# Weight pieces that move in natural-orientation products start 64 bytes later in their buffers

## The chip, the cores and the metric

The kernel runs on one core of a Trainium2 chip. The metric is the device time of one execution in microseconds (us), as the median of several runs. A profile of one execution shows what each engine did: TensorE (PE for matmuls, PEld for the loading of a stationary operand), VectorE (DVE), ScalarE (ACT), GpSimd (POOL), SyncE (SP), and the DMA queues.

## The reference

The reference is a two-layer encoder trunk in float32 on 256 tokens of width 2048. Cut to what matters here:

```python
for layer in range(2):
    h = rmsnorm(x, attn_norm[layer])
    if layer == 0:      # two head groups: chunked attention, differential attention
        qa, ka, va, qb, kb, vb = split(h @ even_w_in)          # 2048 x 6144
        x = x + concat(attn_a(qa, ka, va), attn_b(qb, kb, vb)) @ even_w_out
    else:               # sparse attention on a shared latent c (256 wide), 16 heads
        q, cl, ... = split(h @ odd_w_in); c = rmsnorm(cl)
        # keys of a head are c @ w_uk, its values c @ w_uv
        x = x + attn_c(q, c, w_uk, w_uv) @ odd_w_out
    h = rmsnorm(x, ffn_norm[layer])
    x = x + (silu(h @ w_gate) * (h @ w_up)) @ w_down           # inner width 5632
return rmsnorm(x, final_norm)
```

Nearly all the work is the product of 256 tokens with some 390 MB of float32 weights.

## The kernel before, in words

**Weights in pieces.** A weight matrix comes as pieces of 128 partitions by 1024 columns: two row blocks (j = 0 and 1) of 512 columns each. `sources` is a generator that yields the pieces in the order of their use, and `load_w` takes the next one: SyncE's queue loads it into a buffer `wl` (5 of them), ScalarE writes its rounded copy `wh` in the format float32r, VectorE the remainder `wo = wl - wh`. Of `wh` and of `wo` there are 3 buffers each. `next_w` keeps three pieces ahead. The activations stand in the same split form: `xs` (the normalized input, 16 blocks), `mix` (attention output), `y` (inner activations of the FFN), `c` (the latent), each block as a high half and a low half of 256 tokens.

**Two kinds of product.** In `gemm_t`, `products` makes transposed outputs: the weights are stationary (128 columns are loaded into the array) and the activations move through it. Per piece and output block n this is a group of four matmuls: `wh` of j = 0 and 1 against the high and low halves at once (512 columns move), then `wo` of j = 0 and 1 against the high half (256 columns move). The projections of queries and keys, both output projections, and all of the FFN are made so. In `keys_values` the keys of layer 1 (`uk`) are made in the same way from `w_uk`, with the latent `c` as the moving operand.

In `gemm_n` the outputs are in natural orientation (tokens on partitions; the tile is called `nat`): here 128 tokens of the activations are stationary and the weights move, 512 columns at a time, in three matmuls: activation high by `wh`, high by `wo`, low by `wh`. Only values are made so: the third group of `even_groups` of each of the four head quads of layer 0 (8 pieces each, with `xs`), and `w_uv` in layer 1 (4 pieces, with `c`).

**Order.** The program of PE is a fixed list, written in the order of these calls. Between the matmuls of a gemm `pump` places small steps of the attention. A matmul that 512 columns move through is preceded by a load of its stationary operand, which overlaps the matmul before it.

**Addresses.** Tiles lie at fixed offsets within each partition, in the order in which they are allocated. In the program as built, `xs` begins at byte 32,896, the three `wh` at 89,664 and every 4096 bytes after it, the three `wo` at 101,952 and every 4096 bytes after it. Tiles called `spacer` (88, 8 and 168 floats) move `y` and `mix` to chosen offsets: `y` is at 123,008, `mix` at 180,352 in layer 0 and 170,112 in layer 1; `c` is at 221,376. The slices that the matmuls take start at multiples of 512 bytes from these, except in the small projection `x` (pieces of 656 columns), where those of j = 1 start 1312 bytes in.

Of the kernel before, what the change touches and what calls it, by code (L numbers as in the profile page):

```python
# [14 lines left out]
F32R = mybir.dt.float32r  # L15
# [5 lines left out]
P = 128  # L21
S = 256
D = 2048
KT = D // P
# [15 lines left out]
def encoder_kernel(  # L40
# [25 lines left out]
    wpool = ctx.enter_context(tc.tile_pool(name="wpool", bufs=1))  # L66
# [14 lines left out]
        return psum.tile(shape, F32, name=name, tag="ps")  # L81


    OUT0 = [4, 5, 6, 7, 0, 1, 2, 3]
    QUADS = (2, 3, 0, 1)

    def even_groups(quad):
        return (quad, 2 + quad, 4 + quad) if quad < 2 else (4 + quad, 6 + quad, 8 + quad)

    def ffn_sources(layer):  # L90
        for g in range(FT // 4):
            yield from (w_gate[layer, g, k] for k in range(KT // 2))
            yield from (w_up[layer, g, k] for k in range(KT // 2))
        for g in range(4):
            yield from (w_down[layer, g, k] for k in range(FT // 2))

    def sources():
        for quad in QUADS:
            for g in even_groups(quad):
                yield from (w_ein[g, k] for k in range(KT // 2))  # L100
        for g in range(4):
            yield from (w_eout[g, k] for k in OUT0)
        yield from ffn_sources(0)
        yield from (w_ox[k] for k in range(KT // 2))
        yield from (w_oi[k] for k in range(KT // 2))
        for quad in range(4):
            yield from (w_oq[quad, k] for k in range(KT // 2) if quad)
            yield w_uk[quad]
            yield w_uv[quad]
            yield from (w_oq[quad, k] for k in range(KT // 2) if not quad)  # L110
        for g in range(4):
            yield from (w_oout[g, k] for k in range(KT // 2))
        yield from ffn_sources(1)

    stream = sources()
    ahead = deque()
    latest = {}
    before = deque()

    def load_w(cuts=1, between=None):  # L120
        src = next(stream, None)
        if src is None:
            return
        if before:
            before.popleft()()
        width = src.shape[-1]
        wl = wpool.tile([P, width], F32, name="wl", tag="wl", bufs=5)
        wh = wpool.tile([P, width], F32R, name="wh", tag="wh", bufs=3)
        wo = wpool.tile([P, width], F32R, name="wo", tag="wo", bufs=3)
        for i in range(cuts):  # L130
            if between is not None:
                between(i)
            c = slice(i * width // cuts, (i + 1) * width // cuts)
            nc.sync.dma_start(out=wl[:, c], in_=src[:, c])
            latest["act"] = nc.scalar.activation(wh[:, c], wl[:, c], AF.Copy)  # L135
            nc.vector.tensor_tensor(out=wo[:, c], in0=wl[:, c], in1=wh[:, c].bitcast(F32), op=ALU.subtract)  # L136
        ahead.append((wh, wo))

    def next_w():
        while len(ahead) < 3:  # L140
            n = len(ahead)
            load_w()
            if len(ahead) == n:
                break
        return ahead.popleft()
# [188 lines left out]
    def load_x(t, n):  # L334
        if t:
            nc.sync.dma_start(out=xt[:, t:t + n, :], in_=xT[:, t:t + n, :])
        normalize_tiles(t, n, 0)

    load_w(2, between=lambda i: load_x(i, 1))
    before.extend(partial(load_x, t, 2) for t in range(2, KT, 2))  # L340
    load_w(2)
    load_w(2)

# [3 lines left out]
    def attention_pools(stack, spacer):  # L347
        ap = stack.enter_context(tc.tile_pool(name="attn", bufs=2))
        mixp = stack.enter_context(tc.tile_pool(name="mix", bufs=1))
        mixp.tile([P, spacer], F32, name="spacer")  # L350
        return ap, mixp, mixp.tile([P, KT, 2, S], F32R, name="mix")
# [134 lines left out]
    stack = ExitStack()  # L486
    ap, mixp, mix = attention_pools(stack, 8)
# [55 lines left out]
    for quad in QUADS:  # L543
        qk, ps = {}, []
# [31 lines left out]
    def out_proj(mix, order, gi):  # L576
        st = {"acc": None}
        for g in range(4):
            banks = gemm_t(mix, KT, order)
            if g == 0:  # L580
                drain()
            add_residual(banks, 4 * g, gi, st)
        return st

    st = out_proj(mix, OUT0, 1)
    stack.close()
# [75 lines left out]


    stack = ExitStack()
    ap, mixp, mix = attention_pools(stack, 168)
    hk = mixp.tile([P, C_HEADS, S], F32, name="hk1")
    steps.append(norm_steps(st, "n2", scale))

# [127 lines left out]
    for quad in range(4):  # L796
        qk = {}
# [89 lines left out]
```

## Time and profile before

| what | us |
|---|---|
| median of 3 runs | 2138.07 (2137.47 to 2138.16) |
| the profiled execution's own time | 2138.02 |
| its span, from first to last instruction | 2136.2 |
| PE busy with matmuls | 2122.6 |
| VectorE busy | 1347.7 |
| ScalarE busy | 1067.7 |

The profiled execution's time is its span and 1.8 us around it. The granted clock of TensorE is 0.998 of full speed over the span. The duration that the profile shows for one matmul is longer than its share of the engine's time, since a matmul starts while the one before it drains; how often one starts is read from the starts in the timeline. A row of the timeline joins matmuls that follow one another on the same tiles: its first number is the start of the first of them.

### The profile page before, as it was taken

What the parts mean: (1) busy time and instruction counts of PE and PEld (TensorE: products, weight loads), DVE (VectorE), ACT (ScalarE), POOL (GpSimd) and SP (SyncE); (2) the same over time, 40 slices, a digit from 0 to 9 for tenths busy, and PEclk for the clock granted to TensorE, in tenths of its full rate; (3) what the DMA queues carried; (4) which work ended last, traced back from release to release, by engine and by line L of the source; (5) the groups of instructions that cost most, each with busy time, mean ns of one, the idle gap of its engine ahead of it and who ended that gap; (6) DMA issues with size and microseconds to landing.
All of it is one profiled execution on the core that took longest, in us unless ns stands there. A gap on an engine that the chain in (4) does not pass through costs nothing.

```text
span 2136.2 us, 31865 instructions
## 1 busy us (share of the span) xinstructions
PE 2122.6 (99%) x12280; PEld 1862.8 (87%) x12280; DVE 1347.7 (63%) x1978; ACT 1067.7 (50%) x1575; POOL 231.0 (11%) x232
## 2 busy tenths in 40 slices
PE   9999999999999999999999999999999999999998
PEld 8888888888888888888888888888888888888887
DVE  6665557766666666655547977666666666654444
ACT  6555555545454544444435566454454545444442
POOL 3111001100000000000002242110010000100000
PEclk9999999999999999999999999999999999999999
DMA  8455445555555555555556444655555555555553
GB/s 288 163 179 177 168 168 187 189 195 188 190 193 190 190 194 188 192 192 187 180 185 214 164 160 147 198 188 190 195 188 192 192 189 193 191 189 193 191 190 127
DMA packets 114407, 398.92 MB, mean 187 GB/s; under 512 B 12554, under 2 KB 16718, under 8 KB 114254
## 3 DMA queue, kind: packets, MB, share of 16 engines
q1 hardware_dynamic: 114110, 396.75, 56.0%
q8 instruction: 96, 1.57, 0.3%
q14 instruction: 57, 0.47, 0.1%
q10 hardware_dynamic: 144, 0.13, 0.0%
HBM read 394.70 MB, written 2.14 MB: 186 GB/s over the span
## 4 chain that ended last, share of the span: by engine, by line
PE 95%; DVE 2%; POOL 1%; ACT 1%; issue 1%; DMA 1%; SPq 0%; POOLq 0%; DVEq 0%; ACTq 0%
PE acc L171 86%; PE nat L171 4%; PE x L171 1%; DVE wo L136 1%; DMA xt<-in_xT 1%; POOL sqacc L299 1%; PE uk L171 0%; DVE sc L748 0%; DVE sc L758 0%; ACT wh L135 0%; POOL tm L767 0%; DVE m L757 0%; DVE xt L818 0%; PE c3o L171 0%; DVE qT L318 0%
## 5 line engine op out<-in xcount | busy, mean ns | idle before, releaser
L136 DVE TENSOR_TENSOR wo<-wl,wh 128x1024 fp32r<-128x1024 f32 (+2 forms) x747 | 943.6, 1265 | 727.4 <-ACT wh L135 718.1
L135 ACT ACTIVATE wh<-wl 128x1024 fp32r<-128x1024 f32 (+2 forms) x747 | 785.1, 1051 | 897.1 <-PE acc L171 821.6
L171 PE MATMUL acc<-xs,wh 128*128 128x512 f32 x3648 | 1139.4, 393 | 0.2 <-ACT wh L135 0.2
L171 PEld LDWEIGHTS acc<-xs,wo 128*128 128x128 f32 x3648 | 685.1, 188 | 152.5 <-DVE wo L136 2.0
L171 PE MATMUL acc<-xs,wo 128*128 128x256 f32 x3648 | 722.8, 279 | 1.0 <-DVE wo L136 1.0
L171 PEld LDWEIGHTS acc<-xs,wh 128*128 128x128 f32 x3648 | 554.4, 188 | 3.2 <-ACT wh L135 0.9
L171 PE MATMUL acc<-y,wh 128*128 128x512 f32 x1412 | 437.1, 391 | 0.0
L171 PEld LDWEIGHTS acc<-y,wo 128*128 128x128 f32 x1408 | 264.4, 188 | 58.1
L171 PE MATMUL acc<-y,wo 128*128 128x256 f32 x1408 | 278.3, 279 | 0.0
L171 PEld LDWEIGHTS acc<-y,wh 128*128 128x128 f32 x1412 | 213.8, 188 | 0.0
L171 PE MATMUL acc<-mix,wh 128*128 128x512 f32 x512 | 160.0, 394 | 0.0
L317 ACT ACTIVATE u<-acc 128x256 f32<-128x256 f32 x228 | 86.2, 378 | 60.8 <-PE acc L171 55.8
L171 PEld LDWEIGHTS acc<-mix,wo 128*128 128x128 f32 x512 | 96.1, 188 | 21.3
L171 PE MATMUL acc<-mix,wo 128*128 128x256 f32 x512 | 101.1, 279 | 0.0
L299 POOL TENSOR_TENSOR sqacc<-sqacc,sq 128x512 f32<-128x512 f32 (+1 forms) x36 | 53.4, 1483 | 410.3 <-ACT sq L294 408.2
L171 PE MATMUL nat<-wh,xs 128*128 128x512 f32 x256 | 83.6, 394 | 0.0
L606 POOL TENSOR_TENSOR ga<-ga,n1rs 128x256 f32<-128x256 f32 x44 | 36.6, 843 | 425.4 <-DVE ga L605 411.3
L606 POOL TENSOR_TENSOR ga<-ga,n3rs 128x256 f32<-128x256 f32 x44 | 36.6, 843 | 425.5 <-DVE ga L605 411.2
L171 PEld LDWEIGHTS acc<-mix,wh 128*128 128x128 f32 x512 | 77.7, 188 | 0.2
L171 PEld LDWEIGHTS nat<-wh,xs 128*128 128x128 f32 x256 | 48.0, 187 | 10.8
L305 DVE TENSOR_TENSOR xt<-acc,xt 128x256 f32<-128x256 f32 x120 | 44.6, 418 | 19.1 <-PE acc L171 19.1
L171 PE MATMUL nat<-wo,xs 128*128 128x512 f32 x128 | 50.5, 394 | 0.0
(811 smaller groups left out, 1084.7 us busy)
## 6 DMA issues: line engine op xcount, KB each, us to landing
wl<-in_w_gate SPq DMA_DIRECT2D x176, 512.0 KB, 3.3
wl<-in_w_up SPq DMA_DIRECT2D x176, 512.0 KB, 3.3
wl<-in_w_down SPq DMA_DIRECT2D x176, 512.0 KB, 3.3
wl<-in_w_ein SPq DMA_DIRECT2D x93, 512.0 KB, 3.3
wl<-in_w_eout SPq DMA_DIRECT2D x32, 512.0 KB, 3.3
wl<-in_w_oq SPq DMA_DIRECT2D x32, 512.0 KB, 3.2
wl<-in_w_oout SPq DMA_DIRECT2D x32, 512.0 KB, 3.4
wl<-in_w_oi SPq DMA_DIRECT2D x8, 512.0 KB, 4.3
```

The source lines that it names most:

```text
L135: latest["act"] = nc.scalar.activation(wh[:, c], wl[:, c], AF.Copy)
L136: nc.vector.tensor_tensor(out=wo[:, c], in0=wl[:, c], in1=wh[:, c].bitcast(F32), op=ALU.subtract)
L171: nc.tensor.matmul(out, a, b, start=start, stop=stop, skip_group_check=True)
L299: nc.gpsimd.tensor_tensor(out=st["acc"][:, :n, :], in0=st["acc"][:, :n, :], in1=sq[:, :n, :], op=ALU.add)
L305: nc.vector.tensor_tensor(out=xt[:, t0 + i, :], in0=b[:, part, :], in1=xt[:, t0 + i, :], op=ALU.add)
L317: nc.scalar.activation(u[:m], b[:m, 0, :], AF.Copy)
L606: nc.gpsimd.tensor_tensor(out=a, in0=a, in1=st["rs"], op=ALU.mult)
```

## The change

A piece that `sources` marks gets an offset of 16 floats (64 bytes) within its `wh` and `wo` buffers; each of these buffers grows by 32 floats (128 bytes) so that it has room for that. The marked pieces are the value pieces of layer 0 (the third group of each quad) and `w_uk`. `w_uv` is not marked. The spacer ahead of `mix` in layer 1 falls from 168 to 8 floats.

```diff
+    OFF = 16
...
+    def moving(pieces):
+        return ((src, OFF) for src in pieces)
+
     def sources():
         for quad in QUADS:
-            for g in even_groups(quad):
+            *qk, v = even_groups(quad)
+            for g in qk:
                 yield from (w_ein[g, k] for k in range(KT // 2))
+            yield from moving(w_ein[v, k] for k in range(KT // 2))
...
-            yield w_uk[quad]
+            yield w_uk[quad], OFF
             yield w_uv[quad]
...
+        src, off = src if isinstance(src, tuple) else (src, 0)
...
-        wh = wpool.tile([P, width], F32R, name="wh", tag="wh", bufs=3)
-        wo = wpool.tile([P, width], F32R, name="wo", tag="wo", bufs=3)
+        wh, wo = (wpool.tile([P, width + 2 * OFF], F32R, name=n, tag=n, bufs=3)[:, off:off + width] for n in ("wh", "wo"))
...
-    ap, mixp, mix = attention_pools(stack, 168)
+    ap, mixp, mix = attention_pools(stack, 8)
```

On every engine the instructions stand in the same order as before, with the same waits; only addresses differ. Where the operands of the products start, as built:

| operand | byte before | byte after | after division by 128, left: before, after |
|---|---|---|---|
| `xs` | 32,896 | 32,896 | 0, 0 |
| `y` | 123,008 | 123,776 | 0, 0 |
| `mix`, layer 0 and 1 | 180,352; 170,112 | 181,120; 170,240 | 0, 0 |
| `c` | 221,376 | 221,504 | 64, 64 |
| `wh`, unmarked piece | 89,664; 93,760; 97,856 | 89,664; 93,888; 98,112 | 64, 64 |
| `wo`, unmarked piece | 101,952; 106,048; 110,144 | 102,336; 106,560; 110,784 | 64, 64 |
| `wh` and `wo`, marked piece | as above | as above and 64 | 64, 0 |

## Rows read from the trace of the kernel before

**Rows 1.** The page: busy times, chain that ended last by engine and line.

```profile
PE 2122.6 (99%) x12280; PEld 1862.8 (87%) x12280; DVE 1347.7 (63%) x1978; ACT 1067.7 (50%) x1575; POOL 231.0 (11%) x232
...
PE acc L171 86%; PE nat L171 4%; PE x L171 1%; DVE wo L136 1%; DMA xt<-in_xT 1%; POOL sqacc L299 1%; PE uk L171 0%; DVE sc L748 0%; DVE sc L758 0%; ACT wh L135 0%; POOL tm L767 0%; DVE m L757 0%; DVE xt L818 0%; PE c3o L171 0%; DVE qT L318 0%
```

**Rows 2.** Who PE waited for: us in total, times, longest us.

```profile
PE acc L171 <- DVE wo L136: 1.0, 3, 0.5
...
PE x L171 <- DVE wo L136: 0.4, 1, 0.4
...
PE acc L171 <- ACT wh L135: 0.2, 1, 0.2
```

**Rows 3.** Instructions of the conversions (L135, L136): min/median/max ns, then waits.

```profile
L136 DVE TENSOR_TENSOR wo<-wl,wh x747: 684/1226/2346, 4.6 to 2116.1; 128x1024 fp32r<-128x1024 f32 x183, 128x512 fp32r<-128x512 f32 x2, 128x656 fp32r<-128x656 f32 x2
...
  ACT wh L135: 718.1, 518
...
L135 ACT ACTIVATE wh<-wl x747: 613/1058/1108, 4.0 to 2115.0; 128x1024 fp32r<-128x1024 f32 x183, 128x512 fp32r<-128x512 f32 x2, 128x656 fp32r<-128x656 f32 x2
...
  PE acc L171: 821.6, 547
```

**Rows 4.** Matmuls of the tile nat: count, min/median/max ns, first and last start.

```profile
L171 PE MATMUL nat<-wh,xs x256: 393/394/398, 55.1 to 299.9; 128*128 128x512 f32 x128
...
L171 PE MATMUL nat<-wo,xs x128: 388/394/398, 55.4 to 299.6; 128*128 128x512 f32 x128
...
L171 PE MATMUL nat<-wh,c x32: 390/395/404, 1167.7 to 1298.7; 128*128 128x512 f32 x32
...
L171 PE MATMUL nat<-wo,c x16: 390/393/396, 1167.9 to 1298.4; 128*128 128x512 f32 x16
```

**Rows 5.** Timeline of PE, layer 0: nine natural products, then a score.

```profile
63.42 0.39 PE L171 MATMUL nat<-wh,xs 128*128 128x512 f32 x1
63.65 0.39 PE L171 MATMUL nat<-wo,xs 128*128 128x512 f32 x1
63.88 0.63 PE L171 MATMUL nat<-wh,xs 128*128 128x512 f32 x2
...
65.52 0.38 PE L171 MATMUL b201s<-kT,qT 128*128 128x128 f32 x2
```

**Rows 6.** Timeline of PE, layer 1: three groups of keys, twelve natural products.

```profile
1226.49 0.63 PE L171 MATMUL uk<-c,wh 128*128 128x512 f32 x2
...
1228.58 0.39 PE L171 MATMUL nat<-wh,c 128*128 128x512 f32 x1
...
1231.38 0.39 PE L171 MATMUL acc<-xs,wh 128*128 128x512 f32 x1
```

**Rows 7.** Matmuls of line 171, FFN of layer 0 (500 to 1000 us).

```profile
L171 PE MATMUL acc<-xs,wo x1100: 276/278/283, 499.8 to 878.7; 128*128 128x256 f32 x184
...
L171 PE MATMUL acc<-xs,wh x1098: 388/392/394, 500.0 to 878.4; 128*128 128x512 f32 x183
```

**Rows 8.** Timeline of PE, FFN of layer 0: sixteen matmuls, four groups.

```profile
706.34 0.62 PE L171 MATMUL acc<-xs,wh 128*128 128x512 f32 x2
...
709.10 0.39 PE L171 MATMUL acc<-xs,wh 128*128 128x512 f32 x1
```

**Rows 9.** Timeline of PE, projection x of layer 1: two groups of four.

```profile
1121.72 0.63 PE L171 MATMUL x<-xs,wh 128*128 128x512 f32 x2
...
1123.12 0.40 PE L171 MATMUL x<-xs,wh 128*72 128x512 f32 x1
```

**Rows 10.** The page: costliest groups, matmuls with 512 moving columns.

```profile
L171 PE MATMUL acc<-xs,wh 128*128 128x512 f32 x3648 | 1139.4, 393 | 0.2 <-ACT wh L135 0.2
...
L171 PE MATMUL acc<-y,wh 128*128 128x512 f32 x1412 | 437.1, 391 | 0.0
...
L171 PE MATMUL acc<-mix,wh 128*128 128x512 f32 x512 | 160.0, 394 | 0.0
```

## The prediction

> **What bounds the kernel now.** I read the busy times and the chain of waits on the page first [rows 1]. PE is busy 99% of the span, and the chain that ended last lies on it: 86% in the transposed products (acc), 4% in the natural ones (nat). The other engines feed it and are not waited for: all waits of PE for the conversions of weights together are 1.6 us [rows 2]. ScalarE instead sits idle 821.6 us until PE has given a weight buffer back, and VectorE 718.1 us until ScalarE has written one [rows 3]. So the time is the sum of what one matmul after another takes on PE, and a change of addresses moves the end only if it changes how closely the matmuls follow each other.
>
> Next I looked at whether they follow each other at a rate that depends on addresses. The timeline gives it by the starts. In layer 0 nine natural products take 65.52 - 63.42 = 2.10 us, 233 ns each [rows 5]. In the FFN a group of four transposed products (two of 512 and two of 256 columns) takes (709.10 - 706.34) / 4 = 0.690 us [rows 8]. Two other places have the same group with other addresses. For the keys uk, where the moving latent leaves 64 by 128 and not 0, it takes (1228.58 - 1226.49) / 3 = 0.697 us [rows 6]. For the projection x, where the stationary slice of j = 1 leaves 96, it takes (1123.12 - 1121.72) / 2 = 0.700 us [rows 9]. So where operands start may be worth about 1% of a group; the three places differ in neighbours too, so this is a hint, not a proof.
>
> **The change part by part.** No instruction is added, removed or moved; three things get new addresses.
>
> *Value pieces of layer 0.* 256 + 128 = 384 natural products [rows 4]. Their moving weights began at a remainder (by 128) of 64 and now begin at 0; the stationary `xs` stays at 0. The trace has no natural product with both at 0, so I bound it. The profile's duration of such a matmul is 394 ns in the median [rows 4] where the starts lie 233 apart [rows 5]: some 161 ns of it are the drain, which the next one overlaps, so a difference in duration is a difference in time.
> - Lower end: the shortest matmul of 512 columns in the FFN lasts 388 ns [rows 7]. (394 - 388) x 384 = 2.3 us faster.
> - Upper end: the longest natural product of layer 1 lasts 404 ns [rows 4]. (404 - 394) x 384 = 3.8 us slower.
> - Between them, two rows are near. The natural products of layer 1 have both operands at the same remainder (64), as the changed ones will have: twelve take 1231.38 - 1228.58 = 2.80 us, again 233 ns [rows 6], which means no change. The transposed products of y have the moving operand at 0, as the changed ones will, and last 391 ns in the mean against 393 and 394 for xs and mix [rows 10]; 391 would mean 3 x 384 = 1.2 us faster. I take 0.5 us faster, between these two.
>
> *`w_uk`.* It is stationary in its products, not moving; its slices go from 64 to 0 while `c` stays at 64. There are 64 matmuls, 16 groups. If a group goes from 0.697 to the 0.690 of the FFN, that is 16 x 7 ns = 0.1 us faster; if it goes to the 0.700 of x, 0.05 us slower. I take 0.1 us faster. `w_uv` is not marked and keeps 64 against 64.
>
> *Everything behind the larger buffers.* The six buffers grow by 128 bytes, and `y`, `mix`, `c` and the attention's tiles move. By 128 all moving operands of transposed products still leave 0, and their stationary ones 64. I take no change here and give the other case below. Within a piece the stationary slices lie 512 bytes apart and successive blocks of `xs` 2048, and four groups in a row still average the same 0.690 us [rows 8], so multiples of 512 at least are free.
>
> *Conversions.* ScalarE writes and VectorE reads at the new offsets. I cost this at nothing, since PE's work on a piece hides it: twelve natural products are 12 x 233 ns = 2.80 us, four groups 2.76 us, against a median of 1.06 us on ScalarE and 1.23 us on VectorE [rows 3]. If VectorE took twice as long on a piece it would still be 2.45 us. Only beyond about 2.8 us would PE wait, for the excess.
>
> The sum is 0 - 0.5 - 0.1 = 0.6 us less. Against the profiled execution (span 2136.2, 1.8 us around it, 2138.02 in all, which is the median of 2138.07 but for 0.05) this gives 2137.4 us. With the ends of the first term it is 2135.6 to 2141.8.
>
> By itself: the page "TensorE: Matmul & The Clock Gate" of the Trainium skill (section "Wait — 56ns, not 53.3ns?") gives 215.7 ns from start to start for 512 columns at full clock. If the 64 bytes took away all that natural products need above this, my estimate from that figure is 384 x 17.6 ns = 6.8 us, and the sum would be 2131.2 us. No run here shows 215.7 ns.
>
> **The rivals.**
> - *The addresses do nothing.* The differences between the groups of FFN, uk and x then come from their neighbours (x has loads of 72 columns and uk stands next to scores), and both kinds of natural product at 233 ns, with unequal and with equal remainders, say that no alignment counts. Time: 2138.0 us.
>   The Trainium skill speaks for this rival: "SBUF — State Buffer", section "SBUF: two separate sides", says that TensorE waits on nobody and reads the moving and the stationary operand through two independent ports. By that rule the three groups would not differ by their operands' places; the trace has 0.690, 0.697 and 0.700 us for them, which neither page nor trace explains.
> - *Slower: transposed products lose a fixed distance.* Before, moving and stationary operands of all these products also had fixed remainders by 512: 128 for the moving, 64 for every `wh` and `wo`. After, the three `wh` leave 64, 192, 320 and the three `wo` 448, 64, 192, and `y` and `mix` leave 384 or 256. In each case one buffer in three keeps the old distance of 64. If the distance counts by more than 128 bytes, two thirds of the groups get a worse one. There are (3648 + 1412 + 512) / 2 = 2786 groups [rows 10]. At the price of the nearest row, x instead of FFN, 10 ns: 2786 x 2/3 x 10 ns = 18.6 us, so 2156.6 us. For it: groups do differ by such an amount. Against it: no row has a distance that differs by 128 alone. It decides once a group gets 1.5 ns longer on average (4.3 us over 2786 groups).
> - *Faster: the same mechanism with the other sign.* If the new distances are better, a group may fall to two matmuls of 388 and two of 276 ns [rows 7], less the drain of some 162 each: 2 x (226 + 114) = 680 ns. 2786 x 2/3 x 10 ns = 18.6 us faster, 2119.4 us. A group whose every matmul is the shortest is nowhere in the steady stretches, so this has little behind it.
> - *The marking is wrong for `w_uk`.* It marks a piece that doesn't move, and leaves `w_uv`, which does. Whatever that costs is 64 matmuls, at most 0.1 us either way; it is inside the first case.
>
> **How the numbers follow.** The forecast, 2137.4 us (own range 2135.6 to 2141.8): 0.50. No effect at all, 2138.0: 0.26. Slower by the distance: 0.15. Faster by it: 0.09. The first two lie within 0.2% (4.3 us, about what a measurement of this kernel can tell from no change). So faster 0.09, same 0.76, slower 0.15. The range takes in the first two whole and the near ends of the others, where a smaller price than 10 ns or a smaller share than two thirds would put them: 2134.0 to 2144.5.
>
> **What the changed profile would show.** If the first term is right, the median duration of the natural products of layer 0 goes from 394 to about 393 ns, and twelve of them take about 2.78 us. The groups of uk should fall from 0.697 towards 0.690 us; those of the FFN must stay at 0.690, in both halves of the kernel and whichever buffer a piece lies in. The slower rival would show FFN groups of different length that repeat with every third piece. PE's waits for conversions must stay at 1.6 us. The prediction is wrong if the FFN groups move by more than 1.5 ns, or if natural products move by more than 11 ns, which is 4.3 us over 384.

## The result and the profile after

The changed kernel takes 2164.59 us (median of 4 runs, 2164.17 to 2164.79) against 2137.77 us before (median of 4 runs). The ratio is 1.0125, 95% interval 1.0108 to 1.0143: 27 us slower. The forecast was 2137.4 us, no change; the time lies above the whole range.

The page of the changed kernel, busy times and chain (its lines are numbered 6 higher than before, so L171 is L177):

```profile
span 2162.9 us, 31865 instructions
...
PE 2149.4 (99%) x12280; PEld 1878.6 (87%) x12280; DVE 1344.5 (62%) x1978; ACT 1065.6 (49%) x1575; POOL 231.1 (11%) x232
...
PE acc L177 90%; PE nat L177 5%; PE x L177 1%; DMA xt<-in_xT 1%; PE uk L177 1%; PE is L177 0%; DVE xt L824 0%; PE c3o L177 0%; PE a1o L177 0%; PE a0o L177 0%; PE c0o L177 0%; PE c2o L177 0%; PE c1o L177 0%; DVE wo L142 0%; PE n4p L177 0%
```

The span grew by 26.7 us, and so did PE's busy time (2149.4 against the 2122.6 of [rows 1]). The number of its instructions is the same, and so is the granted clock, 0.998 of full speed. No engine keeps it waiting: these are its waits for conversions, 1.0 + 0.4 + 0.4 = 1.8 us against 1.6 in [rows 2].

```profile
PE acc L177 <- DVE wo L142: 1.0, 3, 0.5
...
PE x L177 <- DVE wo L142: 0.4, 1, 0.4
PE acc L177 <- ACT wh L141: 0.4, 1, 0.4
```

So the same matmuls follow each other less closely. Which ones, the chain in order of time tells. Its pieces are stretches in which PE works without a break: start, length, what, how many matmuls. First the kernel before: twelve natural products, then most of the output projection of layer 0 with the first groups of its FFN, then most of each FFN.

```profile
62.88 2.80 PE nat L171 x12
...
312.29 89.71 PE acc L171 x520
...
405.66 716.22 PE acc L171 x4152
...
1407.27 714.86 PE acc L171 x4144
```

The same stretches of the changed kernel:

```profile
63.01 2.79 PE nat L177 x12
...
66.38 2.77 PE nat L177 x12
...
313.31 91.06 PE acc L177 x520
...
408.06 727.76 PE acc L177 x4152
...
1422.56 726.30 PE acc L177 x4144
```

The two FFNs alone lose 11.5 + 11.4 = 23.0 us of the 26.7. Four matmuls are a group, so 716.22 us over 1038 groups were 690.0 ns each, and 727.76 us are 701.1 ns. Every stretch below is read like this.

The durations agree. In the FFN (500 to 1000 us) the medians of both matmuls of a group rose, 392 to 394 and 278 to 281 ns [rows 7]:

```profile
L177 PE MATMUL acc<-xs,wh x1110: 388/394/398, 499.7 to 888.4; 128*128 128x512 f32 x185
...
L177 PE MATMUL acc<-xs,wo x1110: 278/281/285, 500.2 to 888.7; 128*128 128x256 f32 x185
```

The timeline of the changed kernel's FFN shows where within a stretch. The rows are the first matmuls of groups; by the order of the pieces, the piece that begins at 706.58 lies in the middle one of the three buffers, those that begin at 709.38 and 712.18 in the last and the first:

```profile
706.58 0.63 PE L177 MATMUL acc<-xs,wh 128*128 128x512 f32 x2
...
707.29 0.62 PE L177 MATMUL acc<-xs,wh 128*128 128x512 f32 x2
...
707.99 0.62 PE L177 MATMUL acc<-xs,wh 128*128 128x512 f32 x2
...
708.68 0.62 PE L177 MATMUL acc<-xs,wh 128*128 128x512 f32 x2
...
709.38 0.62 PE L177 MATMUL acc<-xs,wh 128*128 128x512 f32 x2
...
712.18 0.63 PE L177 MATMUL acc<-xs,wh 128*128 128x512 f32 x2
...
715.00 0.63 PE L177 MATMUL acc<-xs,wh 128*128 128x512 f32 x2
```

A piece of four groups took 4 x 0.690 = 2.76 us [rows 8]; it now takes 2.80, 2.80 and 2.82 us. All three buffers lose, but not alike. Averaged over this FFN, from the starts in the trace, the four groups of a piece last 708, 697, 693 and 693 ns in the middle buffer, 702, 700, 707 and 700 ns in the last, and 707, 700, 707 and 700 ns in the first. So the lengths repeat with every third piece, as the slower rival said that they would, and the loss shrinks within each piece of the middle buffer and comes back behind it. The natural products of layer 0, which the change is about, hardly moved: twelve of them took 2.80 us in the chain before and take 2.77 to 2.79 us now.

### The profile page after: what moved, and what is told of

Its sections match the earlier page's. It is cut to its first block, busy times and chain, and to the rows that moved or that the text cites. A ratio compares the mean times of both kernels' runs of the same rounds, so it can differ in the third digit from the quotient of the medians.

```text
span 2162.9 us, 31865 instructions
## 1 busy us (share of the span) xinstructions
PE 2149.4 (99%) x12280; PEld 1878.6 (87%) x12280; DVE 1344.5 (62%) x1978; ACT 1065.6 (49%) x1575; POOL 231.1 (11%) x232
## 4 chain that ended last, share of the span: by engine, by line
PE 99%; DMA 1%; DVE 0%; issue 0%; ACT 0%; SPq 0%; POOLq 0%; POOL 0%; DVEq 0%; ACTq 0%
PE acc L177 90%; PE nat L177 5%; PE x L177 1%; DMA xt<-in_xT 1%; PE uk L177 1%; PE is L177 0%; DVE xt L824 0%; PE c3o L177 0%; PE a1o L177 0%; PE a0o L177 0%; PE c0o L177 0%; PE c2o L177 0%; PE c1o L177 0%; DVE wo L142 0%; PE n4p L177 0%
## 5 line engine op out<-in xcount | busy, mean ns | idle before, releaser
L177 PE MATMUL acc<-xs,wh 128*128 128x512 f32 x3648 | 1147.1, 396 | 0.7 <-ACT wh L141 0.4
L177 PEld LDWEIGHTS acc<-xs,wo 128*128 128x128 f32 x3648 | 685.2, 188 | 160.5 <-DVE wo L142 2.0
L177 PE MATMUL acc<-xs,wo 128*128 128x256 f32 x3648 | 730.8, 281 | 1.0 <-DVE wo L142 1.0
L177 PEld LDWEIGHTS acc<-xs,wh 128*128 128x128 f32 x3648 | 559.7, 188 | 3.8 <-ACT wh L141 1.7
L177 PE MATMUL acc<-y,wh 128*128 128x512 f32 x1412 | 440.4, 393 | 0.0
L177 PEld LDWEIGHTS acc<-y,wo 128*128 128x128 f32 x1408 | 264.5, 188 | 61.5
L177 PE MATMUL acc<-y,wo 128*128 128x256 f32 x1408 | 281.5, 281 | 0.0
L177 PEld LDWEIGHTS acc<-y,wh 128*128 128x128 f32 x1412 | 216.1, 188 | 0.0
L177 PE MATMUL acc<-mix,wh 128*128 128x512 f32 x512 | 160.7, 395 | 0.0
L177 PEld LDWEIGHTS acc<-mix,wo 128*128 128x128 f32 x512 | 96.2, 188 | 21.9
L177 PE MATMUL acc<-mix,wo 128*128 128x256 f32 x512 | 102.3, 281 | 0.0
L177 PE MATMUL nat<-wh,xs 128*128 128x512 f32 x256 | 83.2, 394 | 0.0
L177 PEld LDWEIGHTS acc<-mix,wh 128*128 128x128 f32 x512 | 78.4, 188 | 0.2
L177 PEld LDWEIGHTS nat<-wh,xs 128*128 128x128 f32 x256 | 48.0, 188 | 10.4
L177 PE MATMUL nat<-wo,xs 128*128 128x512 f32 x128 | 50.2, 393 | 0.0
```

Of the source, the lines that this page charges most:

```text
L177: nc.tensor.matmul(out, a, b, start=start, stop=stop, skip_group_check=True)
```

## The experiments

In what follows a remainder is that of a start address by 256 bytes, and "64/192" is a piece whose `wh` leaves 64 and whose `wo` leaves 192. Before, every piece was 64/64, and `xs`, `y` and `mix` left 128. In the changed kernel the three buffers are 64/192, 192/64 and 64/192; `xs`, `y` and the `mix` of layer 0 leave 128, the `mix` of layer 1 leaves 0. A rhythm is a spacing of groups that repeats without change. Theories 1 to 3 are stated in the expectation of experiment 2, A and B in that of experiment 5. Each run is compared with the kernel before on the same chip; intervals are of the ratio.

**1. Growth without marking.**

```diff
-            yield from moving(w_ein[v, k] for k in range(KT // 2))
+            yield from (w_ein[v, k] for k in range(KT // 2))
...
-            yield w_uk[quad], OFF
+            yield w_uk[quad]
```

> The changed kernel with no piece marked: the buffers grow by 128 bytes each and the spacer is 8, but every piece starts at the start of its buffer. All theories put the loss into the transposed products: the profile of the changed kernel has 701 to 704 ns per group against 690 before. They expect 2165 us here, with natural products back from 231 to 233 ns (384 x 2 ns = 0.8 us more than the changed kernel). If the marking itself were the loss, this would be 2138 us.

Measured: 2164.14 us (2163.91 to 2164.56), ratio 1.0123 (1.0106 to 1.0140). The chain of this run: four head quads repeat the natural stretch, of which one row stands here, and the FFN.

```profile
62.99 2.77 PE nat L177 x12
...
407.87 727.76 PE acc L177 x4152
...
1422.37 726.30 PE acc L177 x4144
```

The FFNs take to the hundredth what they take in the changed kernel, so the growth of the buffers, with the spacer that goes with it, is the whole loss. The marking does nothing that can be measured (2164.14 against 2164.59 us). The expectation was wrong on one point: the natural products are at 2.77 us without the marking too.

**2. Moving operands at another distance.** Three spacers, 32 floats different.

```diff
-    ap, mixp, mix = attention_pools(stack, 8)
+    ap, mixp, mix = attention_pools(stack, 40)
...
-            fp.tile([P, 88], F32, name="spacer")
+            fp.tile([P, 56], F32, name="spacer")
...
-    ap, mixp, mix = attention_pools(stack, 168)
+    ap, mixp, mix = attention_pools(stack, 136)
```

> The kernel before with three spacers made 32 floats different, so that y and mix leave 0 by 256 instead of 128; wh and wo all keep 64. Theory 1 (a group is slow where wh and wo of a piece leave different remainders by 256): groups stay at 690 ns, 2138 us. Theory 2 (a product is slow where the distance from its stationary to its moving operand is wrong by 256): the 704 groups of y and 256 of mix change by 10 ns or more, both operands of them being at the distance that the changed kernel has in one of two; 960 x 10 to 24 ns = 10 to 23 us, so 2148 to 2161 us, while groups of xs stay at 690. Theory 3 (buffers that follow each other must leave the same remainder by 256): 2138 us.

Measured: 2140.79 us (2140.22 to 2141.66), ratio 1.0014 (1.0004 to 1.0023). In the FFN

```profile
405.70 717.41 PE acc L171 x4152
...
1408.81 716.04 PE acc L171 x4144
```

each stretch is 1.2 us longer. Only the products of y changed, 352 groups per layer, so they pay 3.4 ns each. Where the moving operand starts does count, but by a third of what theory 2 needs; theories 1 and 3, which had no change, missed as well.

**3. All `wo` 128 bytes further on than `wh`** (`y` and `mix` held at 128 by spacers).

```diff
+        if not padded:
+            padded.append(wpool.tile([P, 32], F32, name="pad", tag="pad", bufs=1))
         wo = wpool.tile([P, width], F32R, name="wo", tag="wo", bufs=3)
```

> The kernel before with 128 bytes of padding between the wh and the wo buffers, and spacers that keep y and mix at 128 by 256: all wh leave 64, all wo 192. Theory 1: every group is slow as in the changed kernel, 702 ns instead of 690: 2786 x 12 ns = 33 us, 2171 us. Theory 2: the same 2171 us, since every wo has the wrong distance. Theory 3: no change, 2138 us.

Measured: 2147.51 us (2147.06 to 2147.90), ratio 1.0044 (1.0029 to 1.0059). All three theories missed. The chain says more than the total:

```profile
98.86 30.50 PE acc L174 x176
...
239.75 36.57 PE acc L174 x208
...
312.87 91.43 PE acc L174 x520
...
408.01 719.68 PE acc L174 x4152
...
1326.94 83.20 PE acc L174 x480
...
1413.84 718.30 PE acc L174 x4144
```

Every piece is 64/192 here, and `mix` of layer 0 and `y` both leave 128 (by 512 both leave 384). Yet a group takes 91.43 us / 130 = 703 ns in the stretch of the output projection and 719.68 us / 1038 = 693 ns in the FFN. The two stretches at 98.86 and 239.75 show it with the same moving tile, `xs`: 30.50 us / 44 = 693 ns and 36.57 us / 52 = 703 ns. The same addresses have two rates, and each holds for dozens of groups up to a thousand.

**4. The changed kernel with `wo` moved on by 128 bytes more**, so that the pairs are 64/64, 192/192, 64/64 (the pad of experiment 3, two spacers by 32 floats).

> The changed kernel with 128 bytes of padding between the wh and the wo buffers, and spacers that keep y and mix at 128 by 256: the three pairs leave 64 and 64, 192 and 192, 64 and 64. Theory 1: groups are back at 690 ns in all three buffers and the natural products keep their 231 ns: 2137 us. Theory 2: groups of the middle buffer are slow, 714 ns at twice the price of one wrong operand, the others 690: 929 x 24 ns = 22 us, 2159 us. Theory 3: as the changed kernel, 2164 us.

Measured: 2139.04 us (2138.51 to 2141.07), ratio 1.0007 (0.9997 to 1.0016).

```profile
404.35 717.37 PE acc L181 x4152
```

A group takes 691 ns. 128 bytes of padding in one place take back the loss (2139.04 against 2137.90 us before, and the interval holds 1), though all buffers keep their size, spacing and marks, which rules out theory 3. Experiments 2 to 4 led to a fourth theory, tested next as theory B.

**5. All pieces 192/64.** 128 bytes of padding ahead of `wh` and 128 ahead of `wo`.

```diff
+        if len(padded) == 0:
+            padded.append(wpool.tile([P, 32], F32, name="pad0", tag="pad0", bufs=1))
         wh = wpool.tile([P, width], F32R, name="wh", tag="wh", bufs=3)
+        if len(padded) == 1:
+            padded.append(wpool.tile([P, 32], F32, name="pad1", tag="pad1", bufs=1))
         wo = wpool.tile([P, width], F32R, name="wo", tag="wo", bufs=3)
```

> The kernel before with 128 bytes of padding ahead of the wh buffers and 128 more ahead of the wo buffers: all wh leave 192 by 256 and all wo 64, as in the middle buffer of the changed kernel; moving operands stay at 128. Theory A (a group's time follows from the remainders of its own operands): the middle buffer's mean in the changed kernel, 697.6 ns, everywhere: 2786 x 7.6 ns = 21 us, 2159 us. Theory B (the same remainders have a fast and a slow steady rhythm; a piece with other remainders than the one before it pushes the rhythm over): without alternation groups stay where they settle in the changed kernel, at 692 to 694 ns, so 2786 x 3 ns = 8 us, 2146 us.

Measured: 2144.88 us (2143.98 to 2145.39), ratio 1.0034 (1.0022 to 1.0046): theory B.

```profile
405.91 719.69 PE acc L176 x4152
```

The pair of the middle buffer runs at 693 ns when it is the only one.

**6. Pairs 64/192, 64/192, 64/64.** Each buffer gets its own tag, and pads go between them.

> The kernel before with padding so that the pairs of wh and wo leave 64 and 192, 64 and 192, 64 and 64 by 256; moving operands stay at 128. Theory A: two thirds of the groups at the 694 ns that this pair has in e3_wo_apart, one third at 690: 2786 x 2/3 x 4 ns = 7 us, 2145 us. Theory B: if the step from 64 and 64 to 64 and 192 pushes the rhythm over, the two apart are at 700 to 707 ns as in the changed kernel: 2786 x 2/3 x 13 ns = 24 us, 2162 us; if only the step from 192 and 64 does, 2145 us. So 2162 us speaks against A, 2145 us decides nothing between them.

Measured: 2143.90 us (2143.33 to 2144.11), ratio 1.0029 (1.0018 to 1.0041).

```profile
405.68 718.53 PE acc L184 x4152
...
1410.25 717.20 PE acc L184 x4144
```

A group takes 692 ns. By itself this decides nothing between A and B, as said before the run. Beside the changed kernel it does: the two share the two pairs 64/192 and differ in the third (64/64 here, 192/64 there), and the times differ by 20.7 us. The two also differ in the marks, which cost nothing (experiment 1), and in the `mix` of layer 1; in the two FFNs, where only the pair counts, it is worth 9.2 + 9.1 = 18.3 us. A third of the groups, some 929, lie in it, and experiment 5 shows that its own rate is 693 ns. In the changed kernel its groups average 698 ns and those of the two pairs 64/192 behind it 702 and 703 ns. So it makes the others slow.

**7. Only the `wh` of the value pieces marked, `wh` buffers grown by 256 bytes.** All unmarked pieces stay 64/64; the marked `wh` leave 128.

```diff
-        wh, wo = (wpool.tile([P, width + 2 * OFF], F32R, name=n, tag=n, bufs=3)[:, off:off + width] for n in ("wh", "wo"))
+        wh = wpool.tile([P, width + 64], F32R, name="wh", tag="wh", bufs=3)[:, off:off + width]
+        wo = wpool.tile([P, width], F32R, name="wo", tag="wo", bufs=3)
```

> The kernel before with only the wh of the value pieces of layer 0 moved on by 64 bytes, and each wh buffer grown by 256 bytes instead of 128, so that all wh and wo of other pieces still leave 64 by 256, and y and mix 128. Both theories: groups at 690 ns everywhere, as before; the 256 natural products with wh at 128 like their stationary xs fall from 233 to 227 to 229 ns as in e4_pairs_alike, 256 x 5 ns = 1.3 us: 2136.6 us.

Measured: 2136.55 us (2136.26 to 2137.37) against 2137.63, ratio 0.9996 (0.9987 to 1.0005).

```profile
63.42 2.78 PE nat L178 x12
...
405.25 716.22 PE acc L178 x4152
...
1406.86 714.86 PE acc L178 x4144
```

The FFNs are back to the hundredth, though one `wh`, all `wo`, `y` and `mix` lie 256 bytes elsewhere by 512. Twelve natural products take 2.78 instead of 2.80 us, less than expected. It is the best version that was tried, 28 us under the changed kernel; that it beats the kernel before is not shown, since the interval holds 1.

**8. One piece marked.** All pieces are 64/192 as in experiment 3 except one, number 161 counted from 0, in the FFN of layer 0; it is 192/64.

```diff
+    MARKED = 161
...
+        off = 32 if len(used) == MARKED else 0
...
+        wh = wpool.tile([P, width + room], F32R, name="wh", tag=f"wh{slot}", bufs=1)[:, off:off + width]
...
+        wo = wpool.tile([P, width + room], F32R, name="wo", tag=f"wo{slot}", bufs=1)[:, off:off + width]
```

> All wh leave 64 and all wo 192 by 256, as in e3_wo_apart (2147.5 us), except one piece of the 704 or so, the second gate piece of the third step of the FFN of layer 0, which is moved on by 128 bytes in its buffers, to 192 and 64. Theory A: that one piece costs at most 4 x 15 ns, so 2147.5 us. Theory B: before it the FFN runs at 694 ns per group, behind it at 703 until something else makes TensorE wait, up to the end of that FFN: 231 pieces of 4 groups x 10 ns = 9 us, 2156.5 us.

Measured: 2157.01 us (2156.28 to 2157.54), ratio 1.0091 (1.0077 to 1.0105): theory B, within 0.5 us. The timeline around the marked piece, first matmuls of groups:

```profile
470.18 0.62 PE L187 MATMUL acc<-xs,wh 128*128 128x512 f32 x2
...
486.12 0.62 PE L187 MATMUL acc<-xs,wh 128*128 128x512 f32 x2
...
488.90 0.62 PE L187 MATMUL acc<-xs,wh 128*128 128x512 f32 x2
...
502.96 0.63 PE L187 MATMUL acc<-xs,wh 128*128 128x512 f32 x2
...
1114.86 0.63 PE L187 MATMUL acc<-y,wh 128*128 128x512 f32 x2
...
1124.70 0.63 PE L187 MATMUL acc<-y,wh 128*128 128x512 f32 x2
```

The marked piece is the one from 486.12 to 488.90. The 23 groups ahead of it take 15.94 us, 693 ns each; the 20 behind it 14.06 us, 703 ns each; and more than 600 us later 14 groups still take 9.84 us, 703 ns each, with remainders that are those from ahead of the marked piece. The marked piece itself takes 2.78 us by these rows, within 2 ns a group of those ahead of it; the slower rhythm begins with the step back from it to 64/192. The chain shows how far it lasts:

```profile
407.25 728.87 PE acc L187 x4152
...
1335.54 84.40 PE acc L187 x480
...
1423.65 718.30 PE acc L187 x4144
```

The FFN stretch of layer 0 is 9.2 us longer than in experiment 3, that of layer 1 equal to the hundredth. Between them the output projection of layer 1 takes 84.40 us here and 83.20 us in experiment 3, 703 and 693 ns a group, though no piece near it is 192/64 and the attention ahead of it ran at 693 ns from 1196 to 1220 us; what set the slower rhythm off there is not shown.

**9 and 10. Even remainders of 128 and of 96.** 64 and 32 bytes of padding ahead of `wh`, spacers so that `y` and `mix` keep 128. The lines are those for 128; for 96 the pad has 8 floats.

```diff
+        if not padded:
+            padded.append(wpool.tile([P, 16], F32, name="pad", tag="pad", bufs=1))
         wh = wpool.tile([P, width], F32R, name="wh", tag="wh", bufs=3)
```

> The kernel before with 64 bytes of padding ahead of the wh buffers: all wh and wo leave 128 by 256, as xs, y and mix do. Both theories let every piece look like the one before it, so one rhythm should hold throughout; neither says which. If the moving and the stationary operand may not start alike, groups go from 690 to 698 to 703 ns (as uk has it, or the slow rhythm): 2786 x 8 to 13 ns = 22 to 36 us, 2160 to 2174 us. If it is only alternation that costs, groups stay within 690 to 694 ns and the 384 natural products, now at 128 like their xs, fall from 233 to 228 ns, 1.9 us: 2136 to 2147 us.

> The kernel before with 32 bytes of padding ahead of the wh buffers: all wh and wo leave 96 by 256, as j = 1 does in the projection x, where a group has 700 ns with j = 0 at 64. If 96 itself is what makes x slow, groups go to 700 ns or more: 2786 x 10 ns = 28 us, 2166 us. If it is the step from 64 to 96 within a group, an even 96 stays within 690 to 694 ns: 2138 to 2149 us.

Measured: 2151.94 us (2151.45 to 2152.16), ratio 1.0066 (1.0051 to 1.0081), at 128; 2146.06 us (2145.92 to 2146.56), ratio 1.0039 (1.0025 to 1.0053), at 96. The chain at 128:

```profile
62.76 2.72 PE nat L174 x12
...
405.10 723.14 PE acc L174 x4152
```

and at 96:

```profile
406.45 719.70 PE acc L174 x4152
```

Groups take 697 ns at 128, between what the two cases gave, and 693 ns at 96, so it is not 96 by itself that makes x slow. Twelve natural products with both operands at 128 take 2.72 us, 227 ns each, the closest seen; but 64/64 with 128 is better for the groups, of which there are far more.

## Why the prediction was wrong, point by point

- **What bounds the kernel** was right: PE's starts set the time, and no other engine or queue took part.
- **The step that failed** is "Everything behind the larger buffers", taken at no change because remainders by 128 were kept. What counts is the remainder by 256. The runs bear this out from both sides: 128 bytes of padding between `wh` and `wo`, with `y` and `mix` held at 128, cost 9.6 us (experiment 3) or win back 25.5 us (experiment 4), while shifts by 256 leave the FFNs equal to the hundredth of a microsecond (experiment 7, with 64/64). The term was not 0 but 27 us.
- **The slower rival** named the place, the transposed products, and that a distance by more than 128 bytes decides; it was given 0.15, and the range stopped short of its time. Its price was 10 ns in two thirds of the groups, 18.6 us; measured in the FFNs are 11.1 ns on average (701.1 against 690.0), with a loss in all three buffers. The count of two thirds looked at `wh` and `wo` apart and by 512, and it does not hold even there: `y`, which leaves 384, keeps the old distance of 64 to the `wh` of one buffer but to no `wo`. By 256 each pair has one of the two at 192, and none keeps both at 64.
- **How it costs** was not in any case of the prediction. No fixed price per address explains it: a pair 64/192 has 693 ns in the FFNs of experiment 3 and 703 ns behind a piece 192/64 (experiment 8). The loss over the kernel before is thus some 3 ns for leaving 64/64, and for most pieces about 10 ns more because the changed kernel alternates 64/192 and 192/64 and so falls into the slower rhythm again in each round of three buffers. Experiments 5 and 6 show this by taking out the step from 192/64 to 64/192 in two ways, experiment 8 by putting one such step in. That the slower rhythm lasts until PE waits for something else is shown in experiment 8 only as far as that it lasts for the rest of one FFN and is gone in the attention behind it; what inside the array or the memory keeps it is open. So is what set it off in the output projections of experiments 3 (layer 0, and already in the stretch at 239.75) and 8 (both layers), where no piece is 192/64: such a step is one trigger, not the only one.
- **Value pieces**: 0.5 us faster was forecast. Twelve products fell from 2.80 to about 2.78 us, so 384 of them by some 0.6 us; but experiment 1 has the same without the marking. The size was right by luck, for the reason was not: it came from the larger buffers, not from the 64 bytes.
- **`w_uk`**: 0.1 us faster was forecast. Three groups take 1242.63 - 1240.55 = 2.08 us now against 2.09 [rows 6]; nothing that counts.

```profile
1240.55 0.62 PE L177 MATMUL uk<-c,wh 128*128 128x512 f32 x2
...
1242.63 0.39 PE L177 MATMUL nat<-wh,c 128*128 128x512 f32 x1
```

- **Conversions** cost nothing, as forecast: their medians are 1.23 and 1.06 us as in [rows 3], and PE's waits for them grew by 0.2 us.
- **The hint that I read and discounted**: groups of 690, 697 and 700 ns in [rows 6, 8, 9]. I took them as neighbours' effects with a chance of 0.26 and as small in the rest. Whether those differences came from addresses is not shown for uk, and for x experiment 10 rules out only 96 by itself. But as long as the rate of the bounding engine may depend on addresses, a change that moves the operands of 2786 groups needs a range that holds such a difference for all of them, 2786 x 10 ns = 28 us.

## What to carry to other kernels

Where TensorE is busy all the time, as here, the start addresses of its operands are part of the schedule: before growing a buffer by a few bytes, list what all later tiles leave by 256, keep it as it was and alike for every buffer of a rotation, and pad to 256 and not to 128. Alike is not enough: experiments 3 and 5, with all pieces alike, still lose 9.6 and 7.3 us. Only this kernel with its float32r products was measured. A per-instruction difference that looks too small to matter (11 ns of 690) has to be multiplied by the number of such instructions behind the allocation, not by the number that the change means. And when the same code with the same addresses runs at two rates in one profile, look for what came before it.

## What the runs showed of the hardware

- The spacing of matmul starts depends on operand addresses by 256 bytes. With moving operands at 128, groups take 690 ns with the weights at 64/64, 693 at 96/96 and in the better rhythm of 64/192 and 192/64, 697 at 128/128, and 703 in the other rhythm of 64/192. With the weights at 64/64, moving operands at 0 give 693 instead of 690. These steady rates, to a tenth 690.0, 693.3, 696.7 and 703.3, lie whole multiples of 3.3 ns apart.
- There can be two steady rhythms at the same addresses (693 and 703 ns), and one piece of 2.78 us pushed PE from one into the other for the 647 us that were left of the stretch (experiment 8). In the changed kernel a piece 192/64 leads back to 693 ns within two groups, and the step from it to 64/192 sets the slower rhythm off again.
- The page "SBUF — State Buffer" of the Trainium skill (section "SBUF: two separate sides") has TensorE read its two operands through independent ports and wait on nobody. Of start addresses this rule says nothing, and by it alone they would not count. Experiment 2 moves nothing but where tiles lie, and the products of y pay 3.4 ns per group, so here they do; whether that is a wait at a port, no run shows.
